# First norm's squares summed on TensorE, six shift chunks on VectorE, silu(c) rows by transposes

## The chip, the core and the metric
One core of a Trainium2 chip runs the whole program as one launch. The metric is the device time of one execution in microseconds; a smaller one is better. The engines are TensorE (PE, with its weight loads PEld), VectorE (DVE), ScalarE (ACT), GpSimd (POOL) and SyncE (SP), which here only issues DMAs. Each engine works through its own instructions in the order in which the program holds them.

## The reference
Two transformer blocks of depth 2 run one after the other on 256 tokens of width 1024. Of this, the change touches the first norm and its modulation in the first layer of the first block:

```python
mx = jnp.split((jax.nn.silu(c) @ w_mod[l] + b_mod[l])[:, None, :], N_MOD, axis=-1)
mz = jnp.split(jax.nn.silu(c_ctx) @ w_mod[l] + b_mod[l], N_MOD, axis=-1)
x = x + 0.5 * mx[2] * swiglu(modulate(rms_norm(x), mx[0], mx[1]), ffn1_w1[l], ffn1_w3[l], ffn1_w2[l])
z = z + 0.5 * mz[2] * swiglu(modulate(rms_norm(z), mz[0], mz[1]), ffn1_w1[l], ffn1_w3[l], ffn1_w2[l])
```

Here rms_norm(x) is x / sqrt(mean(x^2) + eps), and modulate(h, shift, scale) is h * (1 + scale) + shift. x and the context z have 256 tokens each, so 512 columns in all. silu(c) and silu(c_ctx) are two rows of 1024 numbers, and w_mod maps them to nine vectors of 1024, of which number 0 is the shift and number 1 the scale of this norm.

## The kernel before
**Layout.** X holds the activations feature-major: 128 partitions by 8 chunks of the width (k = 0 to 7) by 512 columns, x and z side by side. Every large product is done as three fp32r matmuls (L617 to L619, mm3) on operands split into hi and lo: hi*hi, lo*hi, hi*lo. A weight tile raw is loaded by SP (L561), ScalarE casts it to hi (L593), and VectorE subtracts to get lo (L595).

**Start.** SP issues c_sb, the constants k, four loads of X (two chunks each, L488), and then, in pairs, the first 16 modulation chunks mraw (512 KB each, L682, four buffers) with one weight tile after each pair. ScalarE computes c_act = silu(c) for both rows.

**First norm.** ScalarE squares the eight chunks of X (L798, L804; two buffers), VectorE adds them up (acc, L807), and TensorE sums over the partitions of acc with a column of 1/1024 for four groups of 128 columns (L819). VectorE adds eps (L637), GpSimd takes the power -1/2 (L641), TensorE spreads the result by four transposes (L649), and ScalarE copies that to R (L870). R scales every chunk, so nothing of H exists before it.

**Modulation of this norm.** Chunk n of the 16 is the scale (n even) or the shift (n odd) of k = n // 2. TensorE multiplies it with c_wide in eight small matmuls on four column groups (L764), ScalarE copies the result (L773), TensorE adds up the groups (L775), and VectorE adds the bias (L778).

**Chunks of H.** For every k and each half of the columns, VectorE forms mt = X * scale * R (L846), ScalarE writes H_hi = mt + shift (L849), and VectorE writes H_lo (L851).

**Head of the first FFN.** Three pairs of output tiles are computed together: six banks of PSUM stay open, and for k = 0 to 7 in turn the weight tile of that k (384 KB, 768 columns) is multiplied into all six, 18 matmuls for each k, 144 in all. It needs H of chunk k and the split weights of chunk k. Behind it the other output tiles follow, two banks and 48 matmuls each. The products of later modulation vectors run on VectorE during the FFNs (L723: a product of 128 x 1024 with a running sum, with rows crow = silu of c and c_ctx, loaded at L704 and activated at L708).

**Order.** A scheduler at build time simulates threads with estimated durations (the yields) and writes down one order for each engine. Threads ask for a semaphore (sq_sem 2, sb_sem 2, mt_sem 2, eight banks, four mraw buffers) or an event. On the chip the order is fixed; only the waiting times differ.

## Time and profile before
| | us |
|---|---|
| median of three runs | 2463.69 (2462.83 to 2464.11) |
| profiled execution, its own time | 2465.03 |
| its span, first to last instruction | 2463.1 |
| PE busy | 2421.0 (98%) |
| DVE busy | 1561.5 (63%) |
| ACT busy | 971.8 (39%) |
| POOL busy | 488.6 (20%) |

The page gives the busy share of each engine over the span, the chain of work that ended last, and the costliest groups of instructions. A busy share is a mean over stages; for a change in the first 70 us the timeline and the list of waits of that stretch say more. In a timeline a row is a start, a duration from the first to the last of the instructions merged into it, engine, line and operation, and in brackets the idle time of that engine before it and what ended it. Matmuls overlap, so the price of one is taken from start to start. An fp32 matmul shows as two rows (x8 for four matmuls), an fp32r one or a transpose as one.

### The profile page before, as it was taken

How to read it: one execution, taken by the hardware profiler on the slowest of the kernel's cores; microseconds unless marked ns; L12 is line 12 of the kernel's file. 1: busy time of each engine (PE TensorE's matmuls, PEld its weight loads, DVE VectorE, ACT ScalarE, POOL GpSimd, SP SyncE). 2: the span in 40 equal slices, each digit the busy share in tenths (PEclk: the TensorE clock that was granted, in tenths of full speed). 3: DMA queues.
4: the chain of work that ended last, by engine and by line, in shares of the span. 5: the costliest groups of instructions: out<-in, count | busy, mean ns of one | idle time of the engine just before them, and what ended most of it. 6: DMA issues, size and time to landing. Idle time of an engine off the chain costs nothing.

```text
span 2463.1 us, 38749 instructions
## 1 busy us (share of the span) xinstructions
PE 2421.0 (98%) x15186; PEld 2112.9 (86%) x15186; DVE 1561.5 (63%) x2642; ACT 971.8 (39%) x1624; POOL 488.6 (20%) x492
## 2 busy tenths in 40 slices
PE   7999999999999999999999999999999999999998
PEld 5888888876988888988888877999988999989998
DVE  5887746655667666666552657766667555767654
ACT  4222223545422223332222445644536534446443
POOL 0101011521210101110101223100132422222322
PEclk9999999999999999999999999999999999999999
DMA  7765522220355553355642221555433654435652
GB/s 287 242 194 188 183 96 94 70 68 5 125 183 166 163 175 120 104 181 195 208 143 93 88 94 57 206 183 179 157 126 119 205 172 163 148 118 176 202 186 80
DMA packets 105734, 365.85 MB, mean 149 GB/s; under 512 B 13168, under 2 KB 15376, under 8 KB 105040
## 3 DMA queue, kind: packets, MB, share of 16 engines
q1 hardware_dynamic: 82768, 286.58, 35.0%
q10 hardware_dynamic: 21712, 72.98, 9.1%
q0 software_dynamic: 1072, 3.82, 0.5%
q8 instruction: 119, 1.95, 0.3%
q14 instruction: 63, 0.52, 0.1%
HBM read 360.09 MB, written 1.05 MB: 147 GB/s over the span
## 4 chain that ended last, share of the span: by engine, by line
PE 89%; DVE 4%; issue 3%; POOL 2%; ACT 1%; DMA 1%; SPq 0%; POOLq 0%; DVEq 0%; ACTq 0%
PE bank L617 27%; PE bank L618 27%; PE bank L619 27%; DVE lo L595 1%; PE bank L1585 1%; POOL r L641 1%; DMA raw<-in_dram 1%; PE bank L1613 1%; PE bank L1639 1%; ACT hi L593 1%; POOL lev L1327 0%; PE bank L2041 0%; PE bank L2086 0%; PE bank L764 0%; PE bank L2022 0%
## 5 line engine op out<-in xcount | busy, mean ns | idle before, releaser
L617 PE MATMUL bank<-H_hi,hi 128*128 128x512 f32 (+3 forms) x3000 | 997.7, 334 | 0.7 <-ACT H_hi L861 0.5
L618 PE MATMUL bank<-H_lo,hi 128*128 128x512 f32 (+3 forms) x3000 | 982.3, 328 | 2.0 <-DVE H_lo L851 1.9
L619 PE MATMUL bank<-H_hi,lo 128*128 128x512 f32 (+3 forms) x3000 | 981.3, 328 | 0.6 <-DVE lo L595 0.5
L593 ACT CAST hi<-raw 128x1024 fp32r<-128x1024 f32 (+3 forms) x538 | 543.4, 1023 | 994.1 <-PE bank L618 856.4
L595 DVE TENSOR_TENSOR lo<-raw,hi 128x1024 fp32r<-128x1024 f32 (+3 forms) x538 | 659.0, 1235 | 342.0 <-ACT hi L593 338.1
L617 PEld LDWEIGHTS bank<-H_hi,hi 128*128 128x128 f32 x3000 | 564.8, 189 | 61.0 <-issue 7.7
L619 PEld LDWEIGHTS bank<-H_hi,lo 128*128 128x128 f32 x3000 | 566.2, 189 | 51.8 <-DVE lo L595 1.2
L618 PEld LDWEIGHTS bank<-H_lo,hi 128*128 128x128 f32 x3000 | 566.4, 189 | 51.1 <-DVE H_lo L851 2.5
L617 PE MATMUL bank<-gh,hi 128*128 128x512 f32 (+2 forms) x1119 | 369.4, 330 | 1.0 <-ACT gh L928 1.0
L618 PE MATMUL bank<-gl,hi 128*128 128x512 f32 (+2 forms) x1119 | 369.0, 330 | 0.6 <-POOL gl L930 0.6
L619 PE MATMUL bank<-gh,lo 128*128 128x512 f32 (+2 forms) x1119 | 368.8, 330 | 0.0
L930 POOL TENSOR_TENSOR gl<-f,gh 128x512 fp32r<-128x512 f32 (+2 forms) x136 | 169.4, 1246 | 968.4 <-ACT gh L928 968.4
L723 DVE CUSTOM_DVE_ANT_0 prod<-mraw,crow 128x1024 f32<-128x1024 f32 x224 | 306.7, 1369 | 2.9
L617 PEld LDWEIGHTS bank<-gh,hi 128*128 128x128 f32 x1119 | 211.0, 189 | 22.4 <-ACT gh L928 1.4
L618 PEld LDWEIGHTS bank<-gl,hi 128*128 128x128 f32 x1119 | 211.1, 189 | 22.1 <-POOL gl L930 1.2
L619 PEld LDWEIGHTS bank<-gh,lo 128*128 128x128 f32 x1119 | 211.0, 189 | 20.7
L1028 DVE SCALAR_TENSOR_TENSOR X<-bank,mod,X 128x256 f32<-128x256 f32 x192 | 87.0, 480 | 139.1 <-PE bank L619 139.0
L928 ACT CAST gh<-f 128x512 fp32r<-128x512 f32 (+2 forms) x136 | 68.6, 506 | 145.5 <-DVE f L920 113.1
L913 POOL TENSOR_TENSOR s<-s,rstd 128x272 f32<-128x272 f32 (+1 forms) x44 | 65.0, 1478 | 186.7 <-ACT s L911 186.7
L920 DVE TENSOR_TENSOR f<-s,bank 128x512 f32<-128x512 f32 (+2 forms) x114 | 64.2, 565 | 35.0 <-POOL s L913 29.2
L641 POOL TENSOR_TENSOR r<-v,half 128x2 f32<-128x2 f32 (+3 forms) x43 | 47.0, 1095 | 189.0 <-DVE v L637 177.1
L807 POOL TENSOR_TENSOR acc<-acc,sq 128x256 f32<-128x256 f32 (+1 forms) x33 | 42.0, 1272 | 170.3 <-ACT sq L804 170.3
(281 smaller groups left out, 2000.6 us busy)
## 6 DMA issues: line engine op xcount, KB each, us to landing
raw<-in_dram SPq DMA_DIRECT2D x422, 512.0 KB, 3.5
mraw<-in_dram ACTq DMA_DIRECT2D x128, 512.0 KB, 4.3
raw<-in_dram SPq DMA_DIRECT2D x96, 448.0 KB, 3.3
mraw<-in_dram SPq DMA_DIRECT2D x16, 512.0 KB, 4.4
raw<-in_dram SPq DMA_DIRECT2D x8, 504.0 KB, 3.2
raw<-in_dram SPq DMA_DIRECT2D x8, 384.0 KB, 5.3
crow<-in_dram ACTq DMA_DIRECT2D x3, 1024.0 KB, 6.9
X<-in_dram SPq DMA_DIRECT2D x4, 512.0 KB, 6.1
```

The source lines that it names most:

```text
L593: self.ACT.copy(hi, raw)
L595: self.DVE.tensor_tensor(lo, raw, hi.bitcast(F32), op=ALU.subtract)
L617: self.PE.matmul(ps, a[0], b[0], start=first, stop=False)
L618: self.PE.matmul(ps, a[0], b[1], start=False, stop=False)
L619: self.PE.matmul(ps, a[1], b[0], start=False, stop=last)
L641: self.POOL.tensor_tensor(r[:, :n], v[:, :n], self.half[:, :n], op=ALU.pow)
L723: i = self.DVE.tensor_tensor_reduce(prod, got[c], rows[:, s], 1.0, 0.0, ALU.mult, ALU.add, m[:, s, k:k + 1])
L913: self.POOL.tensor_tensor(s, s, late[1], op=ALU.mult)
L920: self.DVE.tensor_tensor(f, s, pb[:, :w], op=ALU.mult)
L928: self.ACT.copy(hi, f)
L930: self.POOL.tensor_tensor(lo, f, hi.bitcast(F32), op=ALU.subtract)
L1028: self.DVE.scalar_tensor_tensor(o, ps[:, r[0] - r0:r[1] - r0], self.mods[l][i][:, s, m:m + 1], o, ALU.mult, ALU.add)
```

## The change
The squares of the eight chunks are no longer added on VectorE. Each is squared by ScalarE (even m) or VectorE (odd m), and TensorE sums it at once over the partitions into four banks, four matmuls for each chunk (L1134), which accumulate over the chunks. VectorE then reads the four banks one by one (L1105). Two of the four X loads move to ScalarE's queue. Ahead of that, TensorE runs three matmuls of 512 columns on a tile of zeros (L763), and 16 transposes of c_act (L769) spread silu(c) into the rows that VectorE needs; VectorE copies them out (L771). These rows take the place of the load and activation of crow in the first FFN. The shift of k = 2 to 7 is computed on VectorE from these rows (shift0, L796, two products for each chunk), not on TensorE; the weights of these chunks are stored transposed. The scales of all chunks and the shift of k = 0 and 1 stay on TensorE (L786, L807, L810).

```diff
-        if name == "w_mod" and n >= MOD0:
+        if name == "w_mod" and (n >= MOD0 or n > 4 and n % 2):
...
-            nc.sync.dma_start(self.X[:, 2 * h:2 * h + 2, META:], x_in[:, 2 * h:2 * h + 2, :])
+            (nc.sync, nc.scalar)[h % 2].dma_start(self.X[:, 2 * h:2 * h + 2, META:], x_in[:, 2 * h:2 * h + 2, :])
...
             if phase == ("ffn1", 0):
                 yield self.raw_ev[7]
...
+                rows = self.rows0
+            else:
+                rows = gp.tile([128, 2, D], F32, name="crow")
...
 def modulation0(self):
...
+        z = self.gp.tile([128, 128], F32, tag="sb0", name="zero", bufs=2)
+        self.POOL.memset(z, 0.0)
+        ps = yield from self.bank()
+        for i in range(3):
+            self.PE.matmul(ps, z, z[:, 0:1].to_broadcast([128, 512]), start=True, stop=True)
+        self.rows0 = self.gp.tile([128, 2, D], F32, name="crow")
+        for s in range(2):
+            for h in range(2):
+                b = yield from self.bank()
+                for j in range(4):
+                    self.PE.transpose(b[:, 128 * j:128 * j + 128],
+                                      self.c_act[:, 4 * h + j, s:s + 1].to_broadcast([128, 128]), self.ident)
+                self.DVE.tensor_copy(self.rows0[:, s, 512 * h:512 * h + 512], b)
+                self.unbank()
+        self.unbank()
         for n in range(MOD0):
             k, i = n // 2, 1 - n % 2
             yield evs[n]
+            if i == 0 and k > 1:
+                self.spawn(self.shift0(k, got.pop(n)), FIRST)
+                continue
...
+    def shift0(self, k, raw):
+        y = self.mods[0][0][:, :, k]
+        for s in range(2):
+            yield "DVE", 1.38
+            prod = self.gp.tile([128, D], F32, tag="prod", name="prod")
+            self.DVE.tensor_tensor_reduce(prod, raw, self.rows0[:, s], 1.0, self.bmod[:, 0, k:k + 1], ALU.mult, ALU.add,
+                                          y[:, s:s + 1])
+        self.release(self.got0_sem)
+        self.fire(self.mod0_ev[0][k])
...
     def first_norm(self, hev):
         R = self.gp.tile([128, 512], F32, tag="f", name="R", bufs=2)
-        st, done = self.new_stats(512, (0, 128, 256, 384)), Ev()
+        ms = []
+        for t in range(4):
+            ms.append((yield from self.bank()))
+        added = [Ev() for _ in range(KD)]
         for m in range(KD):
-            self.spawn(self.add_stats(st, m, self.X[:, m, META:], self.gp, 5.0 + 1.5 * (m // 2)), FIRST)
-        self.spawn(self.late_rstd(st, R, done), FIRST)
-        yield done
+            self.spawn(self.first_sums(ms, m, added), FIRST)
+        yield from self.wait_all(added)
+        v = self.sm.tile([128, 16], F32, tag="v", name="v")
+        for t in range(4):
+            yield dve(1)
+            self.DVE.tensor_scalar(v[:, t:t + 1], ms[t][:, 0:1], EPS, None, ALU.add)
+            self.unbank()
...
+    def first_sums(self, ms, m, added):
+        self.s.cur.ready += 5.0 + 1.4 * (m // 2)
+        yield self.sq_sem
+        x = self.X[:, m, META:]
+        sq = self.gp.tile([128, 512], F32, tag="s", name="sq", bufs=2)
+        if m % 2:
+            yield dve(512)
+            self.DVE.tensor_tensor(sq, x, x, op=ALU.mult)
+        else:
+            yield act(512)
+            self.ACT.activation(sq, x, AF.Square)
+        if m:
+            yield added[m - 1]
+        yield "PE", 0.5
+        for t in range(4):
+            self.PE.matmul(ms[t][:, 0:1], sq[:, 128 * t:128 * t + 128], self.c1("mean"), start=m == 0, stop=m == KD - 1)
+        self.release(self.sq_sem)
+        self.fire(added[m])
```

TensorE's order from the start of the program to the transposes that spread the norm, before: the modulation of chunk 0 (mraw, then sb), the sums of acc (k_89 is the constants), and the spreading (r) in between.

```order
L764 MATMUL bank<-mraw,c_wide 32x128 x8
L819 MATMUL bank<-k_89,acc 128x1 x4
L775 MATMUL bank<-k_89,sb_174 128x2
L764 MATMUL bank<-mraw,c_wide 32x128 x8
L649 MATMUL bank<-k_89,r 128x128 x2
L775 MATMUL bank<-k_89,sb_192 128x2
L649 MATMUL bank<-k_89,r 128x128 x2
```

The same place now, with the zeros and the transposes of c_act ahead.

```order
L763 MATMUL bank<-zero 128x512 x3
L769 MATMUL bank<-k_89,c_act 128x128 x16
L1134 MATMUL bank<-k_89,sq 128x1 x12
L786 MATMUL bank<-mraw,c_wide 32x128 x8
L1134 MATMUL bank<-k_89,sq 128x1 x8
L807 MATMUL bank<-k_89,sb_233 128x2
L786 MATMUL bank<-mraw,c_wide 32x128 x5
L1134 MATMUL bank<-k_89,sq 128x1 x8
L786 MATMUL bank<-mraw,c_wide 32x128 x3
L807 MATMUL bank<-k_89,sb_249 128x2
L1134 MATMUL bank<-k_89,sq 128x1 x4
L649 MATMUL bank<-k_89,r 128x128 x4
```

Four matmuls became 32, of which 20 stand behind the first modulation group and 12 behind the first part of the second.

VectorE's order in the head, about chunk 4, before: two additions of the bias, mt, H_lo and one split for each chunk.

```order
L778 TENSOR_SCALAR mod_1_103<-bank,k_89 128x2
L846 SCALAR_TENSOR_TENSOR mt<-X,mod_1_103,R 128x256 x2
L595 TENSOR_TENSOR lo_129<-raw_62,hi_128 128x768
L778 TENSOR_SCALAR mod_0_102<-bank,k_89 128x2
L851 SCALAR_TENSOR_TENSOR H_lo<-mt,mod_0_102,H_hi 128x256 x2
```

The same engine now, from the split of chunk 3 to mt of chunk 4 (mod_0_102 is the shift, mod_1_103 the scale).

```order
L595 TENSOR_TENSOR lo_71<-raw_61,hi_70 128x768
L796 ISA prod,mod_0_102<-mraw,crow,k_89 128x1024
L796 ISA mod_0_102 128x1
L810 TENSOR_SCALAR mod_1_103<-bank,k_89 128x2
L796 ISA prod,mod_0_102<-mraw,crow,k_89 128x1024
L796 ISA mod_0_102 128x1
L878 SCALAR_TENSOR_TENSOR mt<-X,mod_1_103,R 128x256 x2
L796 ISA prod,mod_0_102<-mraw,crow,k_89 128x1024
L796 ISA mod_0_102 128x1
L883 SCALAR_TENSOR_TENSOR H_lo<-mt,mod_0_102,H_hi 128x256 x2
```

One of the two additions for each chunk has gone, and two products with their readings of the running sum stand in its place; the split of chunk 4 has moved behind them.

## Rows read from the trace of the kernel before

**Rows 1.** The page's first line.

```profile
span 2463.1 us, 38749 instructions
```

**Rows 2.** Waits of TensorE, 0 to 70 us: total us, times, longest.

```profile
PE bank L764 <- DMA mraw<-in_dram: 12.0, 1, 12.0
PE bank L775 <- ACT sb L773: 0.4, 1, 0.4
```

**Rows 3.** Busy time by stretch: length, PE, PEld, DVE, ACT, POOL, clock, DMA.

```profile
100.00:400.00 300.00, 300.00 (x1350) 245.80 (x1348) 211.06 (x300) 78.88 (x104) 36.06 (x26) 1.00 0.50 163
```

**Rows 4.** Timeline of TensorE, 11 to 17 us: start, duration.

```profile
11.98 1.08 PE L764 MATMUL bank<-mraw,c_wide 128*32 128x128 f32 x16 [11.98 <-DMA mraw<-in_dram]
13.26 1.87 PE L819 MATMUL bank<-k,acc 128*128 128x1 f32 x8 [0.19 <-DVE acc L807]
14.98 0.56 PE L775 MATMUL bank<-k,sb 128*128 128x2 f32 x2
...
16.50 0.69 PE L649 MATMUL bank<-k,r 128*128 128x128 f32 x2
16.98 0.55 PE L775 MATMUL bank<-k,sb 128*128 128x2 f32 x2
```

**Rows 5.** Timeline of SyncE, ScalarE and VectorE, 1 to 26 us.

```profile
1.65 1.98 SPq L488 DMA_DIRECT2D X<-in_dram  x4
...
6.06 0.63 ACT L798 ACTIVATE acc<-X 128x512 f32<-128x512 f32 x1 [3.51 <-DMA X<-in_dram]
...
18.09 0.58 ACT L870 COPY R<-bank 128x512 f32<-128x512 f32 x1 [0.47 <-PE bank L649]
18.71 0.88 DVE L846 SCALAR_TENSOR_TENSOR mt<-X,mod,R 128x256 f32<-128x256 f32 x2
...
20.13 0.22 DVE L778 TENSOR_SCALAR mod<-bank,k 128x2 f32<-128x2 f32 x1 [0.54 <-PE bank L775]
20.27 0.88 DVE L851 SCALAR_TENSOR_TENSOR H_lo<-mt,mod,H_hi 128x256 fp32r<-128x256 f32 x2
...
22.51 0.22 DVE L778 TENSOR_SCALAR mod<-bank,k 128x2 f32<-128x2 f32 x1 [0.58 <-PE bank L775]
...
25.46 0.22 DVE L778 TENSOR_SCALAR mod<-bank,k 128x2 f32<-128x2 f32 x1 [1.06 <-PE bank L775]
```

**Rows 6.** Timeline of TensorE: single rows at the two levels of the clock.

```profile
21.04 0.80 PE L617 MATMUL bank<-H_hi,hi 128*128 128x512 f32 x1
...
25.92 0.64 PE L764 MATMUL bank<-mraw,c_wide 128*32 128x128 f32 x16
26.49 0.50 PE L617 MATMUL bank<-H_hi,hi 128*128 128x512 f32 x1
...
640.94 0.50 PE L819 MATMUL bank<-k,acc 128*128 128x1 f32 x4
641.31 0.36 PE L617 MATMUL bank<-H_hi,hi 128*128 128x256 f32 x1
```

**Rows 7.** Timeline of TensorE: last L775, last matmul of the head, first behind it.

```profile
56.40 0.28 PE L775 MATMUL bank<-k,sb 128*128 128x2 f32 x2
...
67.95 0.40 PE L619 MATMUL bank<-H_hi,lo 128*128 128x512 f32 x1
68.19 0.39 PE L617 MATMUL bank<-H_hi,hi 128*128 128x512 f32 x1
```

**Rows 8.** Two stretches as in rows 3, and what TensorE ran in the second.

```profile
0.00:25.00 25.00, 12.39 (x106) 8.93 (x107) 10.88 (x22) 11.41 (x22) 3.13 (x11) 1.00 0.89 321
...
499.50:502.00 2.50, 2.50 (x13) 2.50 (x13) 1.41 (x3) 0.42 (x1) 0.00 (x0) 0.50 0.13 49
...
499.45 0.57 PE L1367 MATMUL bank<-k_mix,p 128*128 128x4 f32 x2
```

**Rows 9.** Timeline of VectorE: a split, and two products of the later modulation.

```profile
17.70 0.95 DVE L595 TENSOR_TENSOR lo<-raw,hi 128x768 fp32r<-128x768 f32 x1
...
84.00 1.23 DVE L723 CUSTOM_DVE_ANT_0 prod<-mraw,crow 128x1024 f32<-128x1024 f32 x1
...
85.27 1.23 DVE L723 CUSTOM_DVE_ANT_0 prod<-mraw,crow 128x1024 f32<-128x1024 f32 x1
```

More of the change, by code (lines that the diff above doesn't have):

```diff
@@ L699, in modulation @@
                 self.s.cur.ready += WAIT
-            rows = gp.tile([128, 2, D], F32, name="crow")
             if phase == ("ffn1", 0):
                 yield self.raw_ev[7]
-            yield "DMA", 2.9, 0.0
-            self.tc.keep_in_program_order(self.nc.scalar.dma_start(rows.rearrange("p s d -> p (s d)"),
-                                                                   self.cst1[:, slice(*C1.at["crow"])]))
-            self.s.cur.ready += 3.0
-            yield act(2 * D)
-            self.ACT.activation(rows, rows, AF.Silu)
+                rows = self.rows0
+            else:
+                rows = gp.tile([128, 2, D], F32, name="crow")
+                yield "DMA", 2.9, 0.0
+                self.tc.keep_in_program_order(self.nc.scalar.dma_start(rows.rearrange("p s d -> p (s d)"),
+                                                                       self.cst1[:, slice(*C1.at["crow"])]))
+                self.s.cur.ready += 3.0
+                yield act(2 * D)
+                self.ACT.activation(rows, rows, AF.Silu)
             def loader():
@@ L1062, in first_norm @@
         R = self.gp.tile([128, 512], F32, tag="f", name="R", bufs=2)
-        st, done = self.new_stats(512, (0, 128, 256, 384)), Ev()
+        ms = []
+        for t in range(4):
+            ms.append((yield from self.bank()))
+        added = [Ev() for _ in range(KD)]
         for m in range(KD):
-            self.spawn(self.add_stats(st, m, self.X[:, m, META:], self.gp, 5.0 + 1.5 * (m // 2)), FIRST)
-        self.spawn(self.late_rstd(st, R, done), FIRST)
-        yield done
+            self.spawn(self.first_sums(ms, m, added), FIRST)
[5 more added lines that the diff above has]
+            self.unbank()
+        r = self.sm.tile([128, 16], F32, tag="r", name="r")
+        yield "POOL", 0.96
+        self.POOL.tensor_tensor(r[:, :4], v[:, :4], self.half[:, :4], op=ALU.pow)
+        rb = yield from self.spread(r, (0, 128, 256, 384), 512)
+        yield act(512)
+        self.ACT.copy(R, rb)
+        self.unbank()
         for k in range(KD):
@@ L1070, in first_norm @@
                 self.spawn(self.mod_tile(k, R[:, r[0]:r[1]], 256, r[0], hev[r][k], lambda: None, 0, 0, s), FIRST)
+    def first_sums(self, ms, m, added):
[7 more added lines that the diff above has]
+        else:
+            yield act(512)
+            self.ACT.activation(sq, x, AF.Square)
[6 more added lines that the diff above has]
+        self.fire(added[m])
     @staticmethod
```

## Prediction

> **What bounds the kernel now.** I read four views in this order. The list of waits on TensorE over the first 70 us shows one wait that matters: 12.0 us until the first modulation weights land [rows 2]. The table by stretches then shows TensorE busy for 300 of 300 us once it runs [rows 3], so what it does in the first 70 us is handed on to the end, and a microsecond won or lost there is a microsecond of the span of 2463.1 us [rows 1]. The order of both kernels fits that: behind the first FFN's head TensorE's order is unchanged, and the last row that moved on any engine stands in that FFN. So I only have to find when the head is done. The head is 144 products (8 chunks of K, 6 banks, 3 each), and the first matmul behind it starts at 68.19 [rows 7].
>
> The timeline of the front then gives two pieces. **Piece one, up to R.** TensorE sums the squares with four one-column matmuls from 13.26 to 15.13 [rows 4], and R, which scales all chunks, is copied out at 18.09 and done at 18.67 [rows 5]. **Piece two, the head.** From R to the first matmul behind the head it takes 68.19 - 18.67 = 49.5 us, and TensorE is its bound: it has no other wait in that list.
>
> **TensorE's clock.** Up to about 24.6 us rows cost about twice what they cost later: L764 takes 1.08 us for 16 rows at 11.98 and runs from 25.92 to 26.49 later, L617 0.80 at 21.04 [rows 4, 6]. That is the lower level, 1.2 GHz, although the column of granted clock prints 1.00 there; at 499.5 it prints 0.50 [rows 8]. The stretch that stays low, 12 to 21 us, is full of L764, L819, L775 and L649, that is, short matmuls; it ends after 512-column matmuls have begun. At 499.5 it falls while TensorE runs L1367, again short ones [rows 8].
>
> **The change, part by part.**
> Zeros and transposes. The three 512-column matmuls on zeros are two passes each; a pass costs 0.23 at the upper level (50 matmuls between 56.40 and 67.95 [rows 7]), so 6 x 0.46 = 2.8 us at the lower, from about 1.2 to 4.0. The 16 transposes have their price in L649: 0.48 for two at the lower level, 16.50 to 16.98 [rows 4], so 3.9 us, until 7.9. At the other end, at the upper level, they take half, until 6.0; then the first square is late next, since the first quarter of X lands at 6.06 and the square takes 0.63 [rows 5]: 6.8. I take 8.0 for the first sum. Two of the X loads go to ScalarE's queue, ahead of silu(c) there: two issues of 0.5 us (1.98 for four on SP [rows 5]), 1.0 us at the most on silu(c), hidden behind the zeros; if not, the start is 9.0. X can also land earlier, but no sum can start before the transposes are through, and a later mraw is waited for at the third sum. I take nothing for it, and 1 us either way for the range.
>
> Sums on TensorE. Before: 4 matmuls, after the additions on VectorE. Now 32, the same instruction on the same shapes. L819 costs (14.98 - 13.26) / 4 = 0.43 each at the lower level [rows 4]; at the upper, 641.31 - 640.94 = 0.37 for two, 0.19 each [rows 6]. So 32 cost 13.8 us or 6.1 us. All but the first 12 stand in TensorE's order behind or between the modulation groups of chunk 0. Which price? The stretch from 8 us on is made of the rows that stood at the lower level from 12 to 21 us, and the zeros are over by then; so 0.43.
> The Trainium skill, "TensorE: Matmul & The Clock Gate", section "LDWEIGHTS (loading the stationary operand)", has a weight load cost its columns at 1.2 GHz, 107 ns for 128; an estimate from it is 64 loads x 0.107 = 6.8 us at either level, and the sum by it would be +0.5 in place of the +7.5 below. The rows differ with the level (0.43 and 0.19), and they decide.
>
> Now piece one: 8.0 + 13.8 (sums) + 2 x 1.08 (both modulation groups of chunk 0, L764's row) + 2 x 0.43 (L807, as one L819) + 0.4 (TensorE waiting for ScalarE's copy of the second group, today's wait for the same pair [rows 2]) = 25.2. From the end of the sums to R it took 18.67 - 15.13 = 3.5, and the steps are the same but for four small reads of banks in place of one. **R at 28.7, 10.0 later than now.** If the upper level held for the first 12 sums, the wait for the first mraw (it lands near 12.0 [rows 2]) would take most of that back: R at 27.4.
>
> Head. Six of the sixteen modulation groups leave TensorE: six times 0.57 (L764, 25.92 to 26.49) and 0.28 (L775, 56.40): 5.1 us less there [rows 6, 7]. VectorE gets 12 products with 1024 columns, 1.27 each, start to start (84.00 to 85.27 [rows 9]): 15.2 us. Its queue in order, from R to the split of chunk 5, which the last 42 products of the head stand behind: 8 x 0.88 (mt), 7 x 0.88 (H_lo), 5 x 0.95 (splits), 8 x 0.22 (additions, now L810), 15.2 = 34.9 us [rows 5, 9]. It also waits: in chunks 0 and 1, which come as before, 0.54 + 0.58 + 1.06 = 2.2 [rows 5]. So the split is done 37.1 after R, 42 x 0.23 = 9.7 follow on TensorE, 0.2 for the handing over: 47.0 in place of 49.5. **VectorE becomes the bound of the head, and 2.5 of the 5.1 us come through.** Bounds: with TensorE as the bound, 2.4 (R to first product, 21.04 - 18.67 [rows 6]) + 144 x 0.23 + 1.6 (8 products at the lower level) + 10 groups less the four ahead of the head, 6 x 0.85 = 42.2; with VectorE's waits doubled, 49.2.
>
> Hidden. The load and silu of crow leave ScalarE's queue; neither shows among the waits [rows 2], so nothing comes of it. The products for the next modulation (L725) move up ahead of two splits on VectorE; the first up-projection behind the head has 48 products, 11 us, to cover them.
>
> **The sum.** 10.0 - 2.5 = +7.5 us. The profiled execution took 2465.03 (span 2463.1 and 1.9 around it), 1.3 above the median of 2463.69: 2472.5 for such an execution, **2471.2** for the median. With R at 27.4 it is +6.2; with a start at 9.0 and VectorE's waits doubled, +10.7.
>
> **The rivals.**
> *The clock stays up* (not slower). The zeros raise it and TensorE, never idle, keeps it. Then the wait for the first mraw at 12.0 [rows 2] is followed by 0.57 + 20 x 0.19 + 0.57 + 0.4 + 0.6 = 5.9, R comes 2.9 later (its four transposes at half price) at 20.8, and the head has no slow start (1.6): 2.1 - 2.5 - 1.6 = -2.0, 2461.7. Against it: 12 to 21 us, a busy TensorE that stayed at the lower level. It decides from the point where the sums cost under 0.25 each. The Trainium skill's page named above, section "Why this matters for your kernels", asks for just this, to keep TensorE continuously busy; by that rule this rival is the forecast, and the trace does not bear it out for short matmuls.
> *TensorE stays the bound of the head.* VectorE's waits vanish, and splits and sums slip into its gaps: 42.2 in place of 47.0, so +2.7, 2466.4. Against it: 34.9 us of work in a row.
> *The head loses the clock again.* Chunk 4's last six products wait for a split that stands behind five chunks of products on VectorE; TensorE has some 3 us with little else and falls as at 499.5 [rows 8]. The next 8 to 16 products cost 0.2 more: +1.6 to +3.2 on top of 7.5, 2474 or so.
> *Faster.* The clock stays up and TensorE stays the bound: -2.0 - 4.8 = -6.8, 2456.9. It decides only if both hold.
>
> **How the numbers follow.** Forecast 0.52, clock stays up 0.20, TensorE the bound 0.13, clock lost again 0.10, faster 0.05. The first, third and fourth hold 0.75, so the range must reach to the second: 2461.5 to 2475. The forecast's own range is 2468 to 2474.5. A measurement of this kernel can tell about 0.2%, 4.9 us: slower holds the forecast (but 0.03 of it) and the clock lost again, 0.59; same holds the clock staying up, TensorE the bound and that 0.03, 0.36; faster 0.05.
>
> **What would show it.** R (L1112) near 28.7, where 21 speaks for the rival; L1134 at 0.43 each; VectorE without gaps between R and the split of chunk 5; a wait of TensorE for VectorE's lo in chunks 4 and 5; the first matmul behind the head near 75.7; from there on the same stretch lengths as before. The prediction is wrong if L1134 costs 0.2, if the first mraw is no longer waited for, or if a later stretch gives the delay back.

## The result and the profile after

The changed kernel is slower by half a per cent. The prediction had the sign right and the size too small, and the measured time lies above its range.

| | us | ratio to before, 95% interval |
|---|---|---|
| first job: after, median of three | 2476.91 (2474.12 to 2480.91) | 1.0051 [1.0037, 1.0064] |
| first job: before, median of four | 2463.90 | |
| second job: after, median of five | 2478.37 (2474.48 to 2480.71) | 1.0052 [1.0039, 1.0066] |
| second job: before, median of 15 | 2464.38 (2462.11 to 2468.84) | |
| predicted | 2471.2 (2461.5 to 2475.0) | 1.0030 |

A fourth execution of the first job, the profiled one, ran with TensorE's clock held down throughout (granted 0.65, 3360.11 us; with it the median is 2478.91), so the profile after is that of the second job (run e1_again, 2477.36 us in that execution, 2465.03 for before). The page's first line, which answers to [rows 1]:

```profile
span 2475.6 us, 38692 instructions
```

TensorE's timeline of the front and the first matmul behind the head: start, duration, engine, line, operation, and in brackets the idle time before it and what ended it. It answers to [rows 4, 7].

```profile
1.31 4.79 PE L763 MATMUL bank<-zero 128*128 128x512 f32 x6 [1.31 <-POOL zero L760]
6.36 1.93 PE L769 MATMUL bank<-k,c_act 128*128 128x128 f32 x16 [0.26 <-DMA k<-in_dram]
10.43 3.79 PE L1134 MATMUL bank<-k,sq 128*128 128x1 f32 x24 [2.14 <-ACT sq L1129]
...
15.16 3.57 PE L1134 MATMUL bank<-k,sq 128*128 128x1 f32 x16
...
25.11 1.84 PE L1134 MATMUL bank<-k,sq 128*128 128x1 f32 x8
28.98 1.12 PE L649 MATMUL bank<-k,r 128*128 128x128 f32 x4 [2.03 <-POOL r L1109]
...
78.62 0.39 PE L617 MATMUL bank<-H_hi,hi 128*128 128x512 f32 x1
```

ScalarE's timeline: its two X loads, the first square, and the copy into R. It answers to [rows 5].

```profile
0.73 1.00 ACTq L488 DMA_DIRECT2D X<-in_dram  x2
...
9.75 0.63 ACT L1129 ACTIVATE sq<-X 128x512 f32<-128x512 f32 x1 [6.49 <-DMA X<-in_dram]
...
30.13 0.58 ACT L1112 COPY R<-bank 128x512 f32<-128x512 f32 x1 [4.79 <-PE bank L649]
```

TensorE's waits from 0 to 110 us: total, times, longest. They answer to [rows 2].

```profile
PE bank L1134 <- ACT sq L1129: 2.1, 1, 2.1
PE bank L649 <- POOL r L1109: 2.0, 1, 2.0
PE bank L807 <- ACT sb L805: 1.7, 3, 0.8
PE bank L619 <- DVE lo L595: 1.5, 2, 0.9
PE bank L763 <- POOL zero L760: 1.3, 1, 1.3
PE bank L769 <- DMA k<-in_dram: 0.3, 1, 0.3
```

And the stretch of [rows 3], with the same columns:

```profile
100.00:400.00 300.00, 300.00 (x1306) 243.88 (x1305) 215.06 (x302) 79.33 (x103) 36.25 (x26) 1.00 0.52 167
```

Read together: TensorE is done with the transposes at 6.36 + 1.93 = 8.29 us and then stands still until 10.43. It waits for the first square, and the square had waited until 9.75 for the first quarter of X, which landed at 6.06 before [rows 5]. The sums end at 26.95, R at 30.71 (18.67 before), and the first matmul behind the head starts at 78.62 (68.19 before [rows 7]). So R comes 12.0 later, the head is 1.6 shorter (47.9 in place of 49.5), and 10.4 us are handed on. From there TensorE is busy 300 of 300 us as before, and the first use of X on VectorE behind the next norm, at 400.2 us before and 410.6 now, is late by the same 10.4.

### The profile page after: what moved, and what is told of

Same layout as the page of the kernel before. It is cut to its first block, busy times and chain, and to the rows that moved or that the text cites. A ratio compares the mean times of both kernels' runs of the same rounds, so it can differ in the third digit from the quotient of the medians.

```text
span 3358.3 us, 38692 instructions
## 1 busy us (share of the span) xinstructions
PE 3340.0 (99%) x15156; PEld 2629.7 (78%) x15156; DVE 1583.9 (47%) x2664; ACT 976.2 (29%) x1613; POOL 465.9 (14%) x493
## 4 chain that ended last, share of the span: by engine, by line
PE 98%; issue 1%; DVE 1%; POOL 0%; DMA 0%; ACT 0%; POOLq 0%; SPq 0%; DVEq 0%; ACTq 0%
PE bank L617 30%; PE bank L618 29%; PE bank L619 29%; PE bank L1651 1%; PE bank L1679 1%; PE bank L1705 1%; PE bank L1467 1%; PE bank L2088 0%; PE bank L2107 0%; PE bank L664 0%; PE bank L2152 0%; PE bank L2224 0%; PE bank L1134 0%; PE bank L2199 0%; PE bank L649 0%
## 5 line engine op out<-in xcount | busy, mean ns | idle before, releaser
L617 PE MATMUL bank<-H_hi,hi 128*128 128x512 f32 (+3 forms) x3000 | 1244.2, 416 | 0.0
L618 PE MATMUL bank<-H_lo,hi 128*128 128x512 f32 (+3 forms) x3000 | 1230.2, 410 | 0.6 <-DVE H_lo L883 0.6
L619 PE MATMUL bank<-H_hi,lo 128*128 128x512 f32 (+3 forms) x3000 | 1227.2, 410 | 0.0
L617 PEld LDWEIGHTS bank<-H_hi,hi 128*128 128x128 f32 x3000 | 680.8, 227 | 145.3 <-issue 56.0
L619 PEld LDWEIGHTS bank<-H_hi,lo 128*128 128x128 f32 x3000 | 684.7, 228 | 134.2 <-issue 42.0
L618 PEld LDWEIGHTS bank<-H_lo,hi 128*128 128x128 f32 x3000 | 686.0, 229 | 131.3 <-issue 42.9
L619 PE MATMUL bank<-gh,lo 128*128 128x512 f32 (+2 forms) x1119 | 460.4, 412 | 0.0
L617 PE MATMUL bank<-gh,hi 128*128 128x512 f32 (+2 forms) x1119 | 460.3, 412 | 0.0
L618 PE MATMUL bank<-gl,hi 128*128 128x512 f32 (+2 forms) x1119 | 460.1, 411 | 0.1
L619 PEld LDWEIGHTS bank<-gh,lo 128*128 128x128 f32 x1119 | 254.8, 228 | 55.6 <-issue 19.2
L617 PEld LDWEIGHTS bank<-gh,hi 128*128 128x128 f32 x1119 | 254.6, 228 | 55.7 <-issue 18.3
L952 DVE TENSOR_TENSOR f<-s,bank 128x512 f32<-128x512 f32 (+2 forms) x114 | 64.1, 564 | 48.1 <-PE bank L619 29.1
```

Source lines behind the costliest of these rows:

```text
L617: self.PE.matmul(ps, a[0], b[0], start=first, stop=False)
L618: self.PE.matmul(ps, a[0], b[1], start=False, stop=False)
L619: self.PE.matmul(ps, a[1], b[0], start=False, stop=last)
L952: self.DVE.tensor_tensor(f, s, pb[:, :w], op=ALU.mult)
```

## The experiments

Twelve kernels ran, four to a job, each beside the kernel before. The table gives what the head says (from one profiled execution of each kernel) and what the times say (medians of 5 to 11 executions, which differ among themselves by 2.5 to 13 us within one kernel). "Head late by" is the first matmul behind the head against 68.19; "median late by" is against before's median in the same job.

| run | what it is | R done | R to behind head | head late by | median late by | ratio [95%] |
|---|---|---|---|---|---|---|
| before | | 18.67 | 49.5 | 0 | 0 | 1 |
| e1_again | the changed kernel | 30.71 | 47.9 | 10.4 | 14.0 | 1.0052 [1.0039, 1.0066] |
| e2_shift_pe | changed, shift on TensorE | 29.81 | 50.3 | 11.9 | 12.1 | 1.0045 [1.0032, 1.0058] |
| e3_sums_dve | changed, squares added on VectorE | 26.18 | 50.9 | 8.9 | 10.0 | 1.0036 [1.0022, 1.0049] |
| e5_x_on_sp | changed, X on SyncE's queue | 22.12 | 47.5 | 1.5 | 3.2 | 1.0013 [1.0004, 1.0022] |
| e6_sp_no_zeros | e5 without the zeros | 22.84 | 48.1 | 2.8 | 6.7 | 1.0034 [1.0021, 1.0047] |
| e7_sp_shift_pe | e5, shift on TensorE | 22.23 | 51.2 | 5.2 | 5.2 | 1.0025 [1.0017, 1.0034] |
| e8_sp_sums_dve | e5, squares added on VectorE | 21.13 | 47.0 | 0.0 | 4.3 | 1.0018 [1.0008, 1.0028] |
| e9_before_split | before, X on two queues | 22.03 | 50.6 | 4.4 | 2.6 | 1.0012 [1.0003, 1.0021] |
| e10_dve_no_zeros | e8 without the zeros | 19.43 | 49.8 | 1.0 | 0.2 | 1.0001 [0.9992, 1.0010] |
| e11_x0_on_act | changed, the two X queues swapped | 27.39 | 47.0 | 6.2 | 8.2 | 1.0037 [1.0024, 1.0049] |
| e12_sums_alone | before, squares summed on TensorE | 25.30 | 51.5 | 8.6 | 16.0 | 1.0062 [1.0048, 1.0076] |
| e13_delay_alone | before, six dead matmuls behind R | 18.32 | 52.4 | 2.6 | 4.2 | 1.0019 [1.0010, 1.0029] |

Two theories stood against each other at first. A: the loss is R, late because X lands late and the sums cost 0.4 us each. B: it lies behind R, in VectorE's new work in the head.

**e1_again**, the changed kernel itself.

> The changed kernel itself, run again, for a profile that can be laid beside that of before. Theory A, the late R: the copy into R ends near 32 us (18.67 before), some 13 us later, because the first quarter of X lands near 10 us (6.06 before) and the 32 sums cost 0.39 to 0.43 us each; from R to the first matmul behind the head it then takes 47 to 49 us, and the first matmul behind the head starts near 80 us (68.19 before), 12 us later, with nothing to come behind it: +12 us for the whole. Theory B, the head: R comes near 29 us, and the rest of the difference lies behind it, in waits of TensorE for the splits on VectorE or in products at the lower clock: from R to the first matmul behind the head 51 us or more.

R at 30.71 and 47.9 from R to behind the head: A holds for the front. "Nothing to come behind it" does not: this execution lost another 1.9 us after the head (2477.36 - 2465.03 = 12.3, less 10.4), and the medians 3.6.

**e2_shift_pe**, the shift back on TensorE.

```diff
-        if name == "w_mod" and (n >= MOD0 or n > 4 and n % 2):
+        if name == "w_mod" and n >= MOD0:
...
-            if i == 0 and k > 1:
-                self.spawn(self.shift0(k, got.pop(n)), FIRST)
-                continue
```

> The changed kernel, but the six chunks of the first shift vector go back to TensorE (the sums on TensorE, the zeros, the transposes and the split of the X loads stay). Theory A, the late R: R stays where the changed kernel has it (within 0.5 us) and the head takes 49 to 50 us as before, so 0 to 2.5 us slower than the changed kernel. Theory B, the head: the products on VectorE are what costs, so 3 us or more faster than the changed kernel.

The head takes 50.3 in place of 47.9 and starts 0.9 earlier, so the shift on VectorE saves in the head what the prediction said (2.4 for a forecast of 2.5 against 49.5). The 0.9 is not the edit's: the first 12 sums cost 2.9 us in place of 3.8, since here the granted clock is still 1.00 from 12 to 13 us, where it is 0.55 in the changed kernel. B would have had this run 3 us faster or more; it is 1.9 faster by medians that each scatter by 4 to 6, and 1.5 slower by the head. By the head B falls; by the medians neither theory has it right, since A said 0 to 2.5 slower.

**e3_sums_dve**, the additions back on VectorE.

```diff
-        ms = []
-        for t in range(4):
-            ms.append((yield from self.bank()))
...
+        st, done = self.new_stats(512, (0, 128, 256, 384)), Ev()
...
```

> The changed kernel, but the squares of the first norm are added on VectorE as before, with four matmuls at the end instead of 32 (shift on VectorE, zeros, transposes and the split of the X loads stay). Theory A, the late R: 28 matmuls at 0.4 us go, some 11 us of TensorE, part of it given back to the later X: R near 23 us and 7 to 10 us faster than the changed kernel, 3 to 5 us slower than before. Theory B, the head: R comes earlier, but the head stays long: within 4 us of the changed kernel.

R comes at 26.18, not at 23: the additions too begin late, and end at 20.2 (TensorE waits 5.6 for them). And the head, which should have kept its 47.9, takes 50.9. So the median is 4.0 below the changed kernel's, where A said 7 to 10 and B 4 at the most: the time is the one that B gave, for a reason that B did not name. TensorE's timeline at its longest wait in the head, in this run:

```profile
60.37 2.93 PE L619 MATMUL bank<-H_hi,lo 128*128 128x512 f32 x6 [4.23 <-DVE lo L595]
63.09 0.63 PE L617 MATMUL bank<-H_hi,hi 128*128 128x512 f32 x1
```

That is the prediction's rival "the head loses the clock again", though not in the kernel that it was meant for. TensorE waits 4.2 us for the split of chunk 4, and the products behind it cost 0.43 from start to start in place of 0.23; in the stretch 60 to 65 us the granted clock is 0.50.

**e5_x_on_sp**, all four loads of X on SyncE's queue.

```diff
-            (nc.sync, nc.scalar)[h % 2].dma_start(self.X[:, 2 * h:2 * h + 2, META:], x_in[:, 2 * h:2 * h + 2, :])
+            nc.sync.dma_start(self.X[:, 2 * h:2 * h + 2, META:], x_in[:, 2 * h:2 * h + 2, :])
```

> The changed kernel, but all four loads of X are issued by SyncE as before. If the split of these loads over two queues is what makes the first quarter land late, the first square starts near 6.1 us in place of 10.0; the first sum then waits for the 16 transposes (they end near 9.2 us) and not for X, starts near 9.3 in place of 10.7, and R comes 1 to 2 us earlier: 1 to 2 us faster than the changed kernel. If the modulation weights then land late (they stand behind X on that queue), nothing is gained: the same to 1 us.

The largest single effect of all runs, and I had put it at 1 to 2 us: R comes 8.6 earlier and the median drops from 2478.37 to 2467.62. The first square and TensorE's front in this run:

```profile
6.32 0.63 ACT L1129 ACTIVATE sq<-X 128x512 f32<-128x512 f32 x1 [3.65 <-DMA X<-in_dram]
```

```profile
5.90 1.91 PE L769 MATMUL bank<-k,c_act 128*128 128x128 f32 x16
7.65 9.82 PE L1134 MATMUL bank<-k,sq 128*128 128x1 f32 x64
17.39 1.08 PE L786 MATMUL bank<-mraw,c_wide 128*32 128x128 f32 x16
```

The 8.6 come in four parts, from these rows and those of the changed kernel above. The first sum starts 2.8 earlier (7.65 against 10.43). The 32 sums cost 9.8 in place of 12.8 (3.79 + 3.57 + 3.57 + 1.84), 3.0 less, since more of them fall into the stretch before 12 us. Two modulation groups and what belongs to them no longer stand between the sums (16.5 - 12.8 = 3.7): TensorE's order came out otherwise by this one edit. The estimates that the kernel's own scheduler uses for the squares are the same in both (5.0 + 1.4 us for each pair of chunks), so the order was moved by a later step of the build; on what grounds, no run shows. And 0.9 is given back between the last sum and R (4.7 in place of 3.8). So the two words "nc.scalar" cost TensorE's order as well as the landing.

**e9_before_split and e11_x0_on_act** measure that load by itself: before, with the split and nothing else, and the changed kernel with the queues swapped, so that ScalarE's has the first quarter.

```diff
-            nc.sync.dma_start(self.X[:, 2 * h:2 * h + 2, META:], x_in[:, 2 * h:2 * h + 2, :])
+            (nc.sync, nc.scalar)[h % 2].dma_start(self.X[:, 2 * h:2 * h + 2, META:], x_in[:, 2 * h:2 * h + 2, :])
```

> The kernel before, with one edit: the second and fourth quarter of X are loaded by ScalarE's queue, as the changed kernel does it. If the split of the loads is a cost by itself: the first quarter lands near 9.7 us in place of 6.06, the additions on VectorE (seven in a row, 4.7 us) start 3 to 4 us later, R comes 3.5 to 7 us later than 18.67, and the run is that much slower than before. Rival, it is hidden behind the wait for the first modulation weights, which ends at 12.0 us anyway: R within 1.5 us, no difference that can be measured.

```diff
-            (nc.sync, nc.scalar)[h % 2].dma_start(self.X[:, 2 * h:2 * h + 2, META:], x_in[:, 2 * h:2 * h + 2, :])
+            (nc.scalar, nc.sync)[h % 2].dma_start(self.X[:, 2 * h:2 * h + 2, META:], x_in[:, 2 * h:2 * h + 2, :])
```

> The changed kernel with the two queues of the X loads swapped: the first and third quarter on ScalarE's queue, which issues its first load at 0.73 us, the second and fourth on SyncE's, which has two other loads ahead. If the queue that starts first takes nearly all of the transfer time (the second and fourth quarter had it in the changed kernel), the first quarter now lands near 6.5 us in place of 9.7, the first sum waits for the transposes alone (they end at 8.3 us) and R comes 1 to 2 us earlier than in the changed kernel, no more, since the second quarter is then the late one: 1 to 2 us faster. Rival, both queues share evenly: the first quarter lands at 8 us or later, R and the time as in the changed kernel.

The first square of e9, then that of e11:

```profile
9.69 0.63 ACT L798 ACTIVATE acc<-X 128x512 f32<-128x512 f32 x1 [6.43 <-DMA X<-in_dram]
```

```profile
5.20 0.63 ACT L1129 ACTIVATE sq<-X 128x512 f32<-128x512 f32 x1 [1.87 <-DMA X<-in_dram]
```

In e9 R moves from 18.67 to 22.03 and the head is 4.4 late: the wait for the first weights does not hide it (there too the order moved: the first L775 now stands ahead of the sums). By the times it is less, 2.6 by medians and 1.0 in the profiled execution. In e11, whose order is that of the changed kernel, the first quarter lands at 5.2, earlier than in any other run, the first sum starts at 8.54, right behind the transposes, and R is 3.3 earlier than in the changed kernel (1 to 2 expected). The queues of the changed kernel between 2 and 4 us (packets, MB, share of the 16 engines' time) say why. q10 is ScalarE's, which issued at 0.73; q1 is SyncE's, where the first load of X stands third and is issued at 1.65, as it was before [rows 5]:

```profile
q10 hardware_dynamic: 225, 0.45, 90.6%
q1 hardware_dynamic: 38, 0.02, 7.0%
```

What SyncE's queue had to move ahead of X were two small loads, c_sb and k, and they were held up as well. The issues of SyncE's queue between 0 and 2 us (KB, us from issue to landing), before and then in the changed kernel:

```profile
X<-in_dram SPq DMA_DIRECT2D x1, 512.0 KB, 4.4
k<-in_dram SPq DMA_DIRECT2D x1, 137.5 KB, 2.6
```

```profile
X<-in_dram SPq DMA_DIRECT2D x1, 512.0 KB, 8.1
k<-in_dram SPq DMA_DIRECT2D x1, 137.5 KB, 5.0
```

The queue that began 0.9 us earlier took nine tenths of the engines' time, and the first quarter of X, the one for which everything waits, was on the other. The Trainium skill, "DMA: Bandwidth & Descriptors", section "Rules for kernel authors", says that spreading loads over several issuing engines does not help the bandwidth, since they share the same 16 engines; the runs agree and go further, a loss in e9 (4.4 us by the head, 2.6 by medians). I should have weighed that rule and did not.

**e12_sums_alone**, the sums by themselves on the kernel before, no zeros, no transposes.

```diff
-        st, done = self.new_stats(512, (0, 128, 256, 384)), Ev()
...
-        self.spawn(self.late_rstd(st, R, done), FIRST)
-        yield done
+            self.spawn(self.first_sums(ms, m, added), FIRST)
+        yield from self.wait_all(added)
...
```

> The kernel before with one part of the change: the squares of the first norm are summed by 32 matmuls on TensorE (no zeros, no transposes, the shift on TensorE, the X loads on SyncE's queue). The first sum starts behind the first square, near 6.9 us. At the prices of the run without zeros (11.0 us for 32) the sums end near 18, R comes near 22.5 us (18.67 before), the head takes 49.5 to 50.3 us as before: 3.5 to 5 us slower than before. Rival, all up to 12 us runs at 0.2 each: R near 19, within 1 us of before.

Its sums, and two stretches of it (length, PE busy, granted clock, DMA share, GB/s):

```profile
6.84 13.81 PE L1102 MATMUL bank<-k,sq 128*128 128x1 f32 x64 [6.84 <-ACT sq L1097]
```

```profile
8.00:10.00 2.00, 2.00 (x11) 1.00 1.06 414
12.00:14.00 2.00, 2.00 (x11) 1.00 1.04 420
```

13.81 us for 32, 0.43 each: the price that the prediction took from L819 [rows 4], to the hundredth, and all of it at the lower level, though the column prints 1.00. R comes at 25.30 (22.5 expected) and the head is 8.6 late (3.5 to 5 expected), the worst of the parts that ran by themselves. The prediction set the Trainium skill, "TensorE: Matmul & The Clock Gate", section "LDWEIGHTS (loading the stationary operand)" beside that price, with an estimate of 6.8 us from it for the 64 loads; measured were 13.8, loads and matmuls together, twice that. By medians this kernel is 16.0 late; the 7.4 that the head does not explain are taken up below.

**e6_sp_no_zeros**, e5 without the zeros.

```diff
-        z = self.gp.tile([128, 128], F32, tag="sb0", name="zero", bufs=2)
-        self.POOL.memset(z, 0.0)
-        ps = yield from self.bank()
-        for i in range(3):
-            self.PE.matmul(ps, z, z[:, 0:1].to_broadcast([128, 512]), start=True, stop=True)
...
-        self.unbank()
```

> The changed kernel with all four X loads on SyncE's queue, and without the three matmuls on zeros. Theory Z, the zeros are what keeps TensorE at the upper level up to 12 us: the 16 transposes then start when the constants land (near 4 us) and cost 0.24 each in place of 0.12, the 32 sums 0.43 each in place of 0.31 on average; R comes near 26 us in place of 22.1, and the run is 3 to 4 us slower than the same kernel with zeros. Theory N, the level up to 12 us does not hang on them: transposes from 4 to 6 us, the first sum right behind the first square near 6.9 us (7.65 with zeros), R 0.5 to 1 us earlier, and the run the same to 1 us faster.

TensorE's front in this run:

```profile
3.78 3.63 PE L764 MATMUL bank<-k,c_act 128*128 128x128 f32 x16 [3.78 <-DMA k<-in_dram]
7.21 10.97 PE L1128 MATMUL bank<-k,sq 128*128 128x1 f32 x64
```

Without the zeros the transposes cost 0.23 each, with them 0.12 (1.91 for 16): the zeros do put TensorE on its upper level. But they take until 5.9 to do it, and the transposes without them are done at 7.4 all the same. The sums then cost 11.0 in place of 9.8. R is 0.7 later and the head 1.3: by the front, Z in kind, N in size. By medians e6 is 3.5 slower than e5, which is Z's size, but its seven executions lie between 2466.13 and 2476.81, and the profiled one is the fastest of them; what the others lost, no trace shows. Transposes at the lower level do as a start: behind them the sums are 2.8 cheaper than alone (13.81).

**e7_sp_shift_pe**, e5 with the edit of e2.

> The changed kernel with all four X loads on SyncE's queue, and with the six chunks of the shift vector back on TensorE. If the products on VectorE shorten the head as the first two runs say (47.6 to 47.9 us from R to the first matmul behind the head, against 50.3 with the shift on TensorE): R stays at 22.1, the head takes 50 us, the run is 2 to 3 us slower than with the shift on VectorE. Rival, the products on VectorE cost later what they save in the head (the first FFN's other work on VectorE, the next modulation): within 1 us.

R 22.23, head 51.2, 3.6 more than with the shift on VectorE. Medians: 2469.62 and 2467.62, in two jobs whose medians of before differ by 0.05; the intervals of the two ratios overlap. The shift on VectorE is the one part of the change that pays in the head. That it pays in the time is not shown: 2.0 for it here, 1.9 against it between e1 and e2.

**e8_sp_sums_dve and e10_dve_no_zeros**: e5 with the edit of e3, and that again without the zeros.

> The changed kernel with all four X loads on SyncE's queue, and with the squares added on VectorE as before: what is left of the change is the shift on VectorE, the zeros and the transposes. If the 32 sums on TensorE are what is left of the loss: R within 2 us of before's 18.7 (the copies of the transposes, four of 0.62 us, stand ahead of the additions on VectorE), the head 47.6 to 48 us, the first matmul behind it between 66.5 and 69 us (68.19 before, 69.65 with the sums on TensorE): 1 to 3 us faster than that, within 1.5 us of before. Rival, the head breaks as in the run with the split loads (TensorE waits 4.2 us for a split and goes down to 1.2 GHz): head 50 us or more, the same as with the sums on TensorE or slower.

> The changed kernel with the X loads on SyncE's queue, the squares added on VectorE, and without the zeros: what is left is the shift on VectorE, whose rows come from 16 transposes while TensorE waits for the first weights anyway. R: the additions on VectorE share it with four copies of the transposes and end near 14.5 us (13.2 before), R near 20 us (18.67 before, 21.1 with the zeros and copies ahead); the head 47.1 us as with the zeros; the first matmul behind it near 67, 1 us earlier than before. Theory 1, behind the head nothing differs: 1 us faster than before. Theory 2, with the shift on VectorE a run loses some 3 us behind the head (the timed medians so far lie 1 to 4 us above what the head alone says): 2 to 3 us slower than before.

e8: R at 21.13, 2.5 later than before (2 at the most expected), and a head of 47.0 (47.6 to 48 expected); the first matmul behind the head starts at 68.16, where it was before and where it was expected. Its median is 4.3 late all the same (1.5 at the most expected), 1.1 above that of e5. e10 leaves only the shift and its transposes: R 19.43, and the expected 47.1 of head would have made it 1.7 faster than before. The head took 49.8. Here are TensorE's row at its wait in the head of e10, and two stretches there with the columns as above:

```profile
53.67 2.93 PE L619 MATMUL bank<-H_hi,lo 128*128 128x512 f32 x6 [0.94 <-DVE lo L595]
```

```profile
52.00:54.00 2.00, 0.72 (x3) 0.88 0.73 256
54.00:56.00 2.00, 2.00 (x6) 0.50 0.80 248
```

The six products behind the split take 2.93 us, in the changed kernel 1.65 behind the same wait of 0.94 (and in both behind the same 0.78 for sb, 1.3 us earlier). So the same waiting cost the clock in one profiled execution and not in the other; e5, e6, e8 and e11 have the wait of 0.94 too and kept the level. Whether the kernel decides it or the execution is open. e10 equals before (1.0001), no more, and is the best of the variants.

**e13_delay_alone**, dead work behind R. The six matmuls on zeros compute nothing.

```diff
+        z = self.gp.tile([128, 128], F32, tag="sb0", name="zero", bufs=2)
+        self.POOL.memset(z, 0.0)
+        ps = yield from self.bank()
+        yield "PE", 10.0
+        for i in range(6):
+            self.PE.matmul(ps, z, z[:, 0:1].to_broadcast([128, 512]), start=True, stop=True)
+        self.unbank()
```

> The kernel before with six 512-column matmuls on zeros put into TensorE's order behind the copy of R; they compute nothing. What it asks is whether a delay ahead of the head comes out one to one at the end. The six cost 0.8 to 1.6 us each, so the first matmul behind the head starts 5 to 10 us later than 68.19. Theory 1: the timed median is later by the same amount, within 1 us. Theory 2, what runs behind the head depends on where it falls in time: the median is later by 2 us or more than the head.

They take 5.9 us (18.64 to 24.52), but the head is only 2.6 late (5 to 10 expected): the modulation groups behind them cost 0.65 in place of 1.08. The median is 4.2 late, 1.6 more than the head, between the two theories; the profiled execution itself is 1.9 late.

**What runs lose behind the head.** From the head on TensorE's order is that of before, and still "median late by" lies from 1.8 below to 7.4 above "head late by". The shift on VectorE is not it: e10 has it (0.8 below) and e12 has not (7.4 above). Part of this is that the head comes from one execution and the median from others. Within the profiled executions alone the end is late, against the 2465.03 of before (0.7 above its median in the second job), by 12.3 in e1 (head 10.4), 7.0 in e3 (8.9), 1.0 in e9 (4.4), 1.1 in e6 (2.8), 4.6 in e8 (0.0) and 16.8 in e12 (8.6): in most of the twelve a delay shrinks by 0.5 to 3.4 us on its way to the end, and in e1, e5, e8 and e12 it grows. In e12 the profiled execution lost 8.2 there, and 7.2 of it at one place, in the second block's token mixing, where the halves of q are swapped by a small transfer. GpSimd's timeline at that place, of before:

```profile
2165.80 1.02 POOL L2006 TENSOR_TENSOR q<-q,k 128x256 f32<-128x256 f32 x1 [2.72 <-DMA u<-q]
2166.78 0.71 POOL L641 TENSOR_TENSOR r<-v,half 128x2 f32<-128x2 f32 x1
```

of e12:

```profile
2179.68 0.98 POOL L2040 TENSOR_TENSOR q<-q,k 128x256 f32<-128x256 f32 x1 [5.03 <-DMA u<-q]
2180.62 1.68 POOL L641 TENSOR_TENSOR r<-v,half 128x2 f32<-128x2 f32 x1
```

TensorE there, and the stretch around it, also of e12:

```profile
2182.36 0.69 PE L649 MATMUL bank<-k,r 128*128 128x128 f32 x2 [4.39 <-POOL r L641]
```

```profile
2180.00:2190.00 10.00, 7.64 (x41) 0.66 0.15 53
```

That transfer (u<-q) keeps GpSimd waiting 5.0 in place of 2.7 us, r stands behind it on that queue and takes 1.68 itself in place of 0.71, TensorE waits 4.4 for r where it did not wait at all before, and its clock falls on top: 0.66 over 10 us, and 7.9 us to the next pair of L649 in place of 5.2. The pairs of L649 on either side of the place, of before and then of e12, give the loss, 31.6 us from the one to the other in place of 24.4:

```profile
2158.93 0.38 PE L649 MATMUL bank<-k,r 128*128 128x128 f32 x2
2183.36 0.38 PE L649 MATMUL bank<-k,r 128*128 128x128 f32 x2
```

```profile
2168.74 0.38 PE L649 MATMUL bank<-k,r 128*128 128x128 f32 x2
2200.37 0.38 PE L649 MATMUL bank<-k,r 128*128 128x128 f32 x2
```

e8 has the same (waits of 5.04 and 3.58, clock 0.83 over 10 us) and loses 5.3 there. The changed kernel loses 3.8 there (2167.72 to 2195.98), more than all of its excess of 1.9: it reaches the place 8.8 late, 1.6 less than behind the head. TensorE's row and two stretches:

```profile
2179.05 0.43 PE L649 MATMUL bank<-k,r 128*128 128x128 f32 x2 [2.10 <-POOL r L641]
```

```profile
2170.00:2180.00 10.00, 7.90 (x52) 0.98 0.37 122
2180.00:2190.00 10.00, 10.00 (x62) 0.85 0.26 95
```

So in these three executions the excess is made of a wait in the second block and of the fall of the clock behind it; for the medians of the other runs no trace shows what it is made of. Why the transfer is late in one kernel and not in another, when nothing there was changed, stays open: no run was made on it.

## Why the prediction was wrong

Two terms that the prediction put at nothing were not nothing: the X loads on two queues, and what comes behind the head. With the first alone the time would have stayed inside the range (2471.2 + 2.0 at R + 0.9 in the head = 2474.1); the 3.6 us behind the head, by medians, carried it out.

The sum of parts, told as a ladder from before to after; each step is a pair of runs of the table, by the head:

| from | to | part | head |
|---|---|---|---|
| before | e12 | squares summed on TensorE | +8.6 |
| e12 | e7 | zeros and transposes | -3.4 |
| e7 | e5 | shift on VectorE | -3.7 |
| e5 | e1 | X loads on two queues | +9.0 |
| before | e1 | all | +10.4 |

The size of a step hangs on what else is there. The sums cost 8.6 on the kernel before and 1.5 behind the zeros (e8 to e5); the split costs 4.4 on the kernel before (e9) and 9.0 here; the shift pays 3.7 here and 1.5 from e2 to e1.

- **The bound** (TensorE handing on what it does in the first 70 us): right up to 400 us, where what the head is late comes out unchanged. To the end it is not one to one, as told above.
- **The X loads: the step that failed.** "X can also land earlier, but no sum can start before the transposes are through, ... I take nothing for it, and 1 us either way for the range." The first quarter landed at 9.75, 3.7 later than before, the first sum started at 10.43 and not at 8.0, and that was 2.4 of the miss. By e5 the edit as a whole costs 9.0 in the head; the order that came with it was known and is in the sum. I had priced the two issues on ScalarE's queue, and not what two queues do to a transfer that is needed first.
- **Zeros and transposes**: 8.29 for a forecast of 7.9, by luck: two errors cancel. The zeros cost 4.8 and not 2.8, since I took a pass of theirs from L617 [rows 7], whose operands are fp32r (a pass of the zeros takes 0.85 from start to start here and 0.43 at the upper level in e13, L617 0.23); the transposes cost 1.9 and not 3.9, since the zeros had raised the clock.
- **The sums**: 12.8 for 13.8. The price of 0.43 is that of e12. Under the zeros a part of them ran at the upper level, which ended at 12 us.
- **From the first sum to R**: 20.3 for 20.7 (28.7 - 8.0), the groups between included. R at 30.71 for 28.7 is all from the start.
- **The head**: 47.9 for 47.0. The split of chunk 5 was done 38.0 after R for 37.1, and then 9.9 for 9.7. TensorE did come to wait for VectorE, but VectorE is not the bound alone: it is busy 32.4 us for 34.9, and where 2.2 us of waits were forecast and "VectorE without gaps" was the sign, it waits 5.5 for TensorE's modulation sums (L810 for L807, seven times between R and the split). Here too two errors cancel; TensorE is busy 45.2 of the 47.9 us. The wait for lo in chunks 4 and 5 is there (0.94 and 0.59), the fall of the clock behind it is not. First matmul behind the head: 78.62 for 75.7.
- **Behind the head, the other step that failed**: nothing was forecast ("from there on the same stretch lengths as before"), and 1.9 came in the profiled execution, 3.6 by the medians. The place is known in that execution, the swap of q in the second block; the cause stays open. It was named as a way to be wrong only in the other direction ("if a later stretch gives the delay back").
- **The profiled execution adds up**: 2.0 (R) + 0.9 (head) + 1.9 (behind) = 4.8, for 2477.36 against the forecast of 2472.5 for such an execution. The range ended at 2475 because its upper end held a start at 9.0 and VectorE's waits doubled, and nothing for a landing of X that the split could move by more.
- **The rivals.** "The clock stays up" came half true: with the zeros it is up until 12 us and then falls, though TensorE goes on without a gap. The two stretches of e5 (columns as above):

```profile
10.00:12.00 2.00, 2.00 (x20) 1.00 1.03 416
12.00:14.00 2.00, 2.00 (x12) 0.50 1.04 415
```

The Trainium skill, "TensorE: Matmul & The Clock Gate", section "Why this matters for your kernels", asks to keep TensorE continuously busy; that was done in e5 (2.00 of 2.00 us in every stretch from 2 to 18 us), and it did not hold the level through a row of one-column fp32 matmuls. "TensorE stays the bound" (42.2) is out. "The head loses the clock again" did not happen in the profiled execution of the changed kernel and did in those of e3 and e10.

## What to carry to other kernels

Ask of every queue what starts ahead of the load that everything waits for: here a second queue that began 0.9 us earlier took the engines from it, and the order that the build wrote moved with the edit. The first quarter of X landed earliest at the front of the first queue (5.2 in e11), yet R came earlier with all four loads on one queue (22.1 in e5 against 27.4). Take a price only from a row of the same type of operand and the same level of the clock: a sum cost 0.43 alone (e12) and 0.31 behind the zeros (e5). When a change is made of parts, run each on both kernels: in the head one part paid here (3.7 us), two words in a load cost 9.0, and neither number holds without the other parts. And hold the head against the time: a delay of one execution is not the delay of the median.

## What the runs showed of the hardware that was not expected

- Two queues did not share evenly from the start: 225 packets against 38 from 2 to 4 us for the one that began 0.9 us earlier (the 38 are mostly of the small loads c_sb and k), 173 against 134 from 4 to 6 us.
- Dead matmuls can cost less than they take: 5.9 us of zeros behind R delayed the head by 2.6, because what follows ran at the upper level.
- A pass of a 512-column matmul costs 0.43 us in fp32 (the zeros of e13) and 0.23 in fp32r (L617), both from start to start at the upper level.
- A wait of the same length cost the clock in one profiled execution and not in another: 0.94 us in the head, followed by six products in 1.65 us in the changed kernel and in 2.93 in e10.
- The granted clock is printed as 1.00 in stretches at the front whose rows are at the lower level: e12 from 8 to 20 us, at 0.43 for each sum, and the zeros of the changed kernel from 2 to 5 us, at 0.85 a pass. Once the rows have been at the upper level the column prints 0.50 when they fall back (e5 from 12 us), so there it can be believed; until then the price of a row decides.
